# A new beginning for a hybrid decoder layer: early x and weights, unread products, a pinned first norm, and the keys' products on VectorE

## The chip, the cores and the metric

One core of a Trainium2 chip runs the whole kernel. The metric is the device time of one execution in microseconds (us). Engines: TensorE (PE, matmuls), VectorE (DVE), ScalarE (ACT), GpSimd (POOL) and SyncE (SP, which only issues DMAs here). Each engine takes its instructions in its own order and waits for the others through semaphores.

## The reference

One step of one decoder layer on 256 prompt positions and 8 samples of 4 tokens: N = 288 columns in all. D = 2048, all in float32.

```python
h = _rmsnorm(x, norm_pre_mix)
z = h @ w_in                              # shift | pool | gate a | gate b columns
zs_mix = zs + (prev - zs) * mu_shift      # token shift
ya, new_wkv = _rwkv7_branch(zs_mix, ...)  # matrix state per head, 16 heads of 64
yb, new_pool = _pool_branch(zp, ...)      # means over windows of 2, 4, 8, 16, then pool_w
m = sigmoid(zga) * (ya @ w_branch_a) + sigmoid(zgb) * (yb @ w_branch_b)
x = x + _rmsnorm(m @ w_out, norm_post_mix)
f, new_conv = _conv_ffn(_rmsnorm(x, norm_pre_ffn), ...)   # gate and up of 5632, conv of 3, gelu
x = x + _rmsnorm(f, norm_post_ffn)
```

The outputs are x for prompt and samples, and the new shift, matrix, pooling and conv states of both.

## The kernel before

**Dense products.** Activations lie transposed: 16 tiles of 128 channels by 288 columns. Each dense product takes 128 x 128 weight tiles and is made as three matmuls of rounded halves (`three`): high weight by high x (L263), high weight by low x (L264), low weight by high x (L265). The halves are exact splits: the high one is a rounded copy, the low one the rest. Weights come in *units* of four tiles, 256 KB: `load_to` issues their DMA on SP's queue into `raw` (seven buffers); `split_to` makes `whi` on ACT (L202) and `wlo` on DVE (L203), four buffers each. `take` keeps the splits three units ahead of the products and the loads six more. A unit is 12 matmuls.

**The start.** The first norm's factor per column (rstd) is applied after the products, so products can begin before it is known. `first_parts(k)` makes the halves of x part k, `xh` (ACT, with the norm's weight g1 from the table `vec`) and `xl` (DVE). `first_squares(k)` squares part k on ACT and adds it to `acc` on POOL; `rstd_of` turns `acc` into rstd by a product with ones and a RECIPROCAL on DVE. Meanwhile `dense_together(seq_lo, ...)` runs five products side by side: units 0 to 4 use x parts 0 to 3, units 5 to 9 parts 4 to 7, and so on, 20 units in all, 240 matmuls. `x_load(q)` loads x parts 4q to 4q+3. `vec` (165.5 KB) and the constants `con` (557.5 KB: identity, ones, masks, eps) come on ACT's queue.

**Side work.** Everything that isn't a dense product is written as generators in three lanes; `advance` takes one step of every lane after each unit, and a half step of lane 2 within a unit. `startup` is the first of lane 1. Then for four groups g of four heads `front(g)` makes the RWKV operands (`cum`, the decay's cumulative sums; `AR`; `KB`, products of keys `kq` and of `tha`, the second operand, with the inverse decay `eN`, at L621; `rr`), and `late(g)` with `inverse` does the chunked recurrence: `Gm` by TensorE and DVE, `Gm*wr` on POOL, written to DRAM as `dA` by POOL's queue, read back as `Ab` by SP's queue, then a triangular inverse on DVE into `wt`, whose product `W` goes through DRAM again (`dW`) and is transposed on DVE (`tq`), for the products `ps_q`, `ps_x` (S), `ps_s` (UV) and `ps_u` (X). Lane 3 makes the pooling branch, `zb`, window sums `win` on POOL, `d` on DVE, its halves `dh` and `dl`, and the branch's `ybh`, `ybl`.

**The second norm.** `rstd_spread` turns sums of squares into a factor spread over 128 partitions: `ps_sum` on TensorE, a square root on ACT, `rq` and the diagonal `dg` on DVE, `ps_spread` on TensorE. It is called for `rst2` between the output product and the feed-forward.

**Order.** A scheduler that simulates the program sets each engine's order by its own estimate, except for instructions wrapped in `pin`, which keep the order in which they are written on their engine. So an edit in one place can move rows elsewhere.

Of the kernel before, what the change touches and what calls it, by code (L numbers as in the profile page):

```python
# [10 lines left out]
F32 = mybir.dt.float32  # L11
# [7 lines left out]
P = 128  # L19
D = 2048  # L20
KD = D // P
# [18 lines left out]
UK = 4  # L40
AHEAD = 3
FA = 2
TOG = 3
BT = 5
IWAIT = 3
# [62 lines left out]
def hybrid_step(ctx: ExitStack, tc: tile.TileContext, t):  # L108
# [69 lines left out]
    def load_to(u):  # L178
        while cursor["load"] <= min(u, len(units) - 1):
            i = cursor["load"]  # L180
            if i in (4, 4 + 5, 4 + 10):
                x_load((i - 4) // 5 + 1)
            ap, nk = units[i]
            m = ap.shape[2]
            w = wp.tile([P, UK, P], F32, tag="raw", name="raw", bufs=7)
            if i:
                nc.sync.dma_start(out=w[:, :nk, :m], in_=ap)
            raw[i] = w
            cursor["load"] += 1
# [127 lines left out]
    con = cst.tile([P, NCON], F32, name="con")  # L317
    xe = ExitStack()
    xr_p = xe.enter_context(tc.tile_pool(name="xr", bufs=1, side="right"))
    nc.scalar.dma_start(out=vec, in_=t["vec"])  # L320
    first = cst.tile([P, 1], F32, name="first")
    dve.memset(first, 0.0)
    act.activation(out=first, in_=first, func=AF.Square)
    nc.scalar.dma_start(out=con, in_=t["con"])
    xr = []

    def x_load(q):
        xq = xr_p.tile([P, 4, N], F32, name=f"xr{q}")
        xr.extend(xq[:, i] for i in range(4))
        if q == 0:  # L330
            load_to(0)
            nc.sync.dma_start(out=xq[:, 0:2], in_=t["xT"][:, 0:2, :])
            nc.sync.dma_start(out=raw[0][:, 0:4], in_=units[0][0][:, 0:4])
            nc.sync.dma_start(out=xq[:, 2:4], in_=t["xT"][:, 2:4, :])
            load_to(1)
        else:
            for h in range(0, 4, 2):
                nc.sync.dma_start(out=xq[:, h:h + 2], in_=t["xT"][:, 4 * q + h:4 * q + h + 2, :])
# [7 lines left out]
    def c_(name):  # L346
        o, w = CON[name]
        return con[:, o:o + w]
# [19 lines left out]
    def rstd_of(sums, name, where):  # L368
        ps = psb.tile([P, 512], F32, tag="s", name="ps_rstd")
        for i, a in enumerate(sums):  # L370
            pe.matmul(ps[:, :N], ones, a, start=i == 0, stop=i == len(sums) - 1)
        r = where.tile([P, N], F32, tag=f"rstd_{name}", name=f"rstd_{name}")
        act.activation(out=r, in_=ps[:, :N], func=AF.Sqrt, scale=1.0 / D, bias=c_("eps"))
        dve.reciprocal(r, r)
        return r

    TC = N // 3

    def rstd_spread(sums, where, between=()):

        ps = psb.tile([P, 3, 2], F32, tag="s", name="ps_sum")
        for i, a in enumerate(sums):
            for c in range(3):
                pin(pe.matmul(ps[0:TC, c], a[:, c * TC:(c + 1) * TC], ones[:, 0:2],
                              start=i == 0 and c == 0, stop=i == len(sums) - 1 and c == 2))
            if i < len(between):
                between[i]()
        q = where.tile([TC, 3, 1], F32, tag="rq", name="rq")
        pin(act.activation(out=q, in_=ps[0:TC, :, 0:1], func=AF.Sqrt, scale=1.0 / D, bias=c_("eps")[0:TC]))
        pin(dve.reciprocal(q, q))  # L390
        dg = where.tile([TC, 3, TC], F32, tag="dg", name="dg")
        pin(dve.tensor_tensor(
            dg, ident[0:TC, 0:TC].unsqueeze(1).to_broadcast([TC, 3, TC]), q.to_broadcast([TC, 3, TC]), op=ALU.mult
        ))
        pr = psb.tile([P, 512], F32, tag="s", name="ps_spread")
        pin(pe.matmul(pr[:, :N], ones[0:TC], dg.rearrange("p c t -> p (c t)"), start=True, stop=True))
        return pr[:, :N]


# [4 lines left out]
    def first_parts(k):  # L404
        xh[k], xl[k] = scaled_parts(k, xr[k], v_("g1", k))

    def first_squares(k):
        if k == 0:
            act.activation(out=acc, in_=xr[0], func=AF.Square)
            return  # L410
        sq = xr_p.tile([P, N], F32, tag="sq", name="sq", bufs=3)
        act.activation(out=sq, in_=xr[k], func=AF.Square)
        pool.tensor_tensor(acc, acc, sq, op=ALU.add)

    def startup():
        for k in range(4, KD, 2):
            first_parts(k)
            first_parts(k + 1)
            yield
        for k in range(KD):  # L420
            first_squares(k)
            if k % 2:
                yield
        norms["mix"] = rstd_of([acc], "mix", cst)

    first_parts(0)
    split_to(0)
# [104 lines left out]
    def front(g, rr, kx, vv, lora):  # L532
# [82 lines left out]
        KBs = kp.tile([P, G, 2, 32], F32, tag="KBs", name="KBs")  # L615
        rh = kp.tile(W2, F32R, tag="t0", name="rh")
        rl = kp.tile(W2, F32R, tag="t3", name="rl")
        for par in range(2):
            for eng, src, flip in ((dve, kq, 0), (pool, bb, 1)):
                h, slot = HALF[par], par ^ flip  # L620
                ins = eng.tensor_tensor(  # L621
                    KB[h, :, :, slot, :].rearrange("p c g t -> p g c t"),
                    src[h, :, :TP].rearrange("p g (c t) -> p g c t", c=NCH),
                    eN[h, :, :TP].rearrange("p g (c t) -> p g c t", c=NCH),
                    op=ALU.mult,
                )
                if eng is dve:
                    pin(ins)
            if not par:
                yield  # L630
        for slot, src in enumerate((kq, bb)):
            pool.tensor_tensor(KBs[:, :, slot, :], src[:, :, TP:], eN[:, :, TP:], op=ALU.mult)
        ready[g] = (vv, AR, KB, KBs, wr, dch, dsm)
# [21 lines left out]
    def late(g):  # L655
# [65 lines left out]
        S0 = kp.tile([P, G, NB, C], F32, tag="S0", name="S0")  # L721
        nc.sync.dma_start(out=S0, in_=t["st_wkv"][:, p0:p0 + G])
        def inverse():
            yield 2 * IWAIT
            pin(dve.memset(Ab.rearrange("p a b -> p (a b)")[:, 0:1024:33], 1.0))
            wt = kp.tile([P, 2, 8, 32], F32, tag="inv", name="wt")
            Wb, tmp = wt[:, 0], wt[:, 1]
            dve.tensor_copy(Wb, c_("inv0").rearrange("p (a b) -> p a b", a=8))
            work = 0
            for tt in range(1, 32):  # L730
                n = tt + 1
                dve.tensor_tensor(  # L732
                    tmp[:, :, :n], Wb[:, :, :n], Ab[:, :n, tt].unsqueeze(1).to_broadcast([P, 8, n]), op=ALU.mult
                )
                dve.tensor_reduce(out=Wb[:, :, tt], in_=tmp[:, :, :n], op=ALU.add, axis=AX.X)
                work += 120 + 16 * n
                if work >= IWORK:
                    yield work // IWORK
                    work %= IWORK
            WQ.dma_start(  # L740
                out=dW.rearrange("q (r i) t -> (q r) (i t)", r=4), in_=Wb.rearrange("p i t -> p (i t)")
            )
# [249 lines left out]
        lane3.todo.append(finish())  # L992

    bones_r = zp_.tile([P, P], F32R, name="bones_r")
    act.copy(out=bones_r, in_=c_("bones"))
    mB = [dmb.tile([P, N], F32, tag=f"mB{j}", name=f"mB{j}") for j in range(16)]
    tga = [dmb.tile([P, N], F32, tag=f"tga{j}", name=f"tga{j}") for j in range(16)]

# [218 lines left out]
        act.activation(out=o, in_=ps[:, :N], func=AF.Copy, scale=v_("g2", j))  # L1217
        og.append(o)
    me.close()
    rst2 = rstd_spread([acc2, sq], ep)  # L1220
    acc3 = ep.tile([P, N], F32, tag="accn3", name="acc3")
    xh, xl = [None] * KD, [None] * KD

# [258 lines left out]
```

## Time and profile before

| What | Value |
|---|---|
| Time, median of 3 runs | 1649.15 us (1648.79 to 1650.57) |
| The profiled execution | 1651.69 us, span 1649.6 us |
| Mean granted clock of TensorE | 0.992 |
| Busy: PE, DVE, ACT, POOL | 1611.8 (98%), 1103.4 (67%), 816.8 (50%), 369.7 (22%) us |
| DMA | 278.96 MB, mean 169 GB/s |
| Chain that ended last | PE 86%, DVE 4%, DMA 2% |

The profile is of one execution; 2.1 us of its time lie outside the span. A row of instructions names line, engine, operation, output and inputs; "[2.22 <-DMA raw<-in_w_in]" says that the engine stood idle for 2.22 us before it, until that event. The granted clock is 1.00 at full speed. Busy time of TensorE includes matmuls that run slowly.

### The profile page before, as it was taken

The page shows a single profiled execution, that of the slowest core. Times are in us where ns is not written, and L with a number is a line of the kernel's source. Part 1 is how long each engine was busy: PE and PEld are TensorE (multiplying, and loading weights), DVE is VectorE, ACT ScalarE, POOL GpSimd, SP SyncE. Part 2 cuts the span into 40 slices and gives each one's busy share as a digit, 9 for nine tenths or more (in the row PEclk, how much of TensorE's full clock was granted, in tenths as well). Part 3 has the DMA queues.
Part 4 walks back from the last instruction along what each step waited for, and adds up shares of the span by engine and source line. Part 5 has one row for each costly group of instructions (what it writes and reads, how often), then busy time and mean ns, then how long its engine had stood idle before and what let it go on. Part 6 is the DMA issues. An engine that isn't in the chain of part 4 may idle for free.

```text
span 1649.6 us, 35997 instructions
## 1 busy us (share of the span) xinstructions
PE 1611.8 (98%) x13540; PEld 1577.3 (96%) x13540; DVE 1103.4 (67%) x2217; ACT 816.8 (50%) x1521; POOL 369.7 (22%) x612
## 2 busy tenths in 40 slices
PE   6989999999999999999999999999999999999998
PEld 6989989989989999999899999999999999999998
DVE  6788887888878766645876664446666555666654
ACT  5544445445435445545655554445555433455554
POOL 4574352343332112300211110001111000111111
PEclk9999999999999999999999999999999999999999
DMA  7535546546545648755355555555555555555553
GB/s 241 161 120 165 170 142 200 161 122 190 157 155 181 187 155 288 229 166 190 108 163 167 167 165 167 166 167 165 168 167 166 166 166 167 166 167 167 176 167 108
DMA packets 157230, 278.96 MB, mean 169 GB/s; under 512 B 25584, under 2 KB 32240, under 8 KB 157056
## 3 DMA queue, kind: packets, MB, share of 16 engines
q1 hardware_dynamic: 151104, 259.16, 50.8%
q0 software_dynamic: 5664, 16.77, 2.9%
q8 instruction: 106, 1.74, 0.4%
q10 hardware_dynamic: 288, 0.74, 0.1%
q14 instruction: 68, 0.56, 0.1%
HBM read 262.67 MB, written 13.93 MB: 168 GB/s over the span
## 4 chain that ended last, share of the span: by engine, by line
PE 86%; DVE 4%; DMA 2%; issue 1%; POOL 0%; ACT 0%; SPq 0%; DVEq 0%; POOLq 0%; ACTq 0%
PE acc L265 27%; PE acc L263 27%; PE acc L264 27%; DVE wlo L203 1%; DMA dW<-wt 1%; PE ps_g L671 0%; DVE xl L357 0%; DVE og L1229 0%; PE ps_s L909 0%; DMA W<-dW 0%; PE ps_u L899 0%; PE ps_x L888 0%; PE ps_y L1353 0%; DVE cum L577 0%; DMA raw<-in_w_in 0%
## 5 line engine op out<-in xcount | busy, mean ns | idle before, releaser
L203 DVE TENSOR_TENSOR wlo<-raw,whi 128x512 fp32r<-128x512 f32 x928 | 661.1, 715 | 415.2 <-ACT whi L202 406.7
L202 ACT CAST whi<-raw 128x512 fp32r<-128x512 f32 x928 | 572.0, 620 | 680.6 <-PE acc L264 629.7
L263 PE MATMUL acc<-xh,whi 128*128 128x288 f32 x2736 | 814.3, 298 | 14.5 <-ACT whi L202 8.8
L265 PE MATMUL acc<-xh,wlo 128*128 128x288 f32 x2736 | 811.4, 297 | 7.0 <-DVE wlo L203 7.0
L264 PE MATMUL acc<-xl,whi 128*128 128x288 f32 x2736 | 812.7, 297 | 0.0
L263 PEld LDWEIGHTS acc<-xh,whi 128*128 128x128 f32 x2736 | 517.4, 189 | 17.9 <-ACT whi L202 9.2
L265 PEld LDWEIGHTS acc<-xh,wlo 128*128 128x128 f32 x2736 | 520.2, 190 | 12.0 <-DVE wlo L203 8.9
L264 PEld LDWEIGHTS acc<-xl,whi 128*128 128x128 f32 x2736 | 520.6, 190 | 2.0 <-issue 0.9
L265 PE MATMUL acc<-ah,wlo 128*128 128x288 f32 x704 | 208.7, 296 | 0.0
L263 PE MATMUL acc<-ah,whi 128*128 128x288 f32 x704 | 208.0, 296 | 0.0
L264 PE MATMUL acc<-al,whi 128*128 128x288 f32 x704 | 205.2, 292 | 0.0
L1266 POOL COPY cout<-gt 128x2 f32<-128x2 f32 x44 | 31.1, 706 | 597.2 <-DVE gt L1262 575.9
L264 PEld LDWEIGHTS acc<-al,whi 128*128 128x128 f32 x704 | 134.2, 191 | 0.0
L263 PEld LDWEIGHTS acc<-ah,whi 128*128 128x128 f32 x704 | 132.2, 188 | 0.0
L265 PEld LDWEIGHTS acc<-ah,wlo 128*128 128x128 f32 x704 | 131.9, 187 | 0.0
L1274 POOL TENSOR_TENSOR cv<-cv,rstd_ffn 128x288 f32<-128x288 f32 x44 | 36.2, 823 | 74.5 <-ACT cv L1273 73.6
L732 DVE TENSOR_TENSOR wt<-wt,Ab 128x16 f32<-128x16 f32 (+30 forms) x124 | 51.4, 414 | 1.8
L462 POOL TENSOR_TENSOR df<-zt 128x256 f32<-128x256 f32 (+1 forms) x27 | 22.7, 840 | 91.6 <-DVE zt L460 85.6
L1270 DVE SCALAR_TENSOR_TENSOR cv<-gt,vec,cv 128x255 f32<-128x255 f32 x88 | 43.0, 489 | 0.0
L263 PE MATMUL acc<-ybh,whi 128*128 128x288 f32 x128 | 38.6, 301 | 0.0
L265 PE MATMUL acc<-ybh,wlo 128*128 128x288 f32 x128 | 38.4, 300 | 0.0
L264 PE MATMUL acc<-ybl,whi 128*128 128x288 f32 x128 | 38.1, 298 | 0.0
(308 smaller groups left out, 1539.8 us busy)
## 6 DMA issues: line engine op xcount, KB each, us to landing
raw<-in_w_ffn_in SPq DMA_DIRECT2D x352, 256.0 KB, 3.0
raw<-in_w_in SPq DMA_DIRECT2D x264, 256.0 KB, 3.5
raw<-in_w_ffn_out SPq DMA_DIRECT2D x176, 256.0 KB, 2.7
raw<-in_w_out SPq DMA_DIRECT2D x64, 256.0 KB, 3.0
raw<-in_w_branch_b SPq DMA_DIRECT2D x32, 256.0 KB, 3.2
raw<-in_w_branch_a SPq DMA_DIRECT2D x32, 256.0 KB, 3.9
xr<-in_xT SPq DMA_DIRECT2D x8, 288.0 KB, 5.6
tga<-th POOLq DMA_DIRECT2D x16, 144.0 KB, 3.7
```

The source lines that it names most:

```text
L202: act.copy(out=hi[:, a:b, :m], in_=w[:, a:b, :m])
L203: dve.tensor_tensor(lo[:, a:b, :m], w[:, a:b, :m], hi[:, a:b, :m].bitcast(F32), op=ALU.subtract)
L263: pe.matmul(ps, hi, xh, start=start, stop=False)
L264: pe.matmul(ps, hi, xl, start=False, stop=False)
L265: pe.matmul(ps, lo, xh, start=False, stop=stop)
L462: pool.tensor_tensor(df[:m, :TP], zt[:m, 0:TP], zt[:m, 1:ZB], op=ALU.subtract)
L732: dve.tensor_tensor(tmp[:, :, :n], Wb[:, :, :n], Ab[:, :n, tt].unsqueeze(1).to_broadcast([P, 8, n]), op=ALU.mult)
L1266: pool.tensor_copy(cout[:, f, 0:2], gt[:, TP - 2:TP])
L1270: dve.scalar_tensor_tensor(cv[:, s:TP], gt[:, 0:TP - s], w, cv[:, s:TP], op0=ALU.mult, op1=ALU.add)
L1274: pool.tensor_tensor(cv, cv, rst3, op=ALU.mult)
```

## The change

- **Unread products.** POOL clears a 128 x 128 tile; TensorE's queue begins with eleven float32 products of it (`WARM`), whose output nothing reads. `keep_busy(n)` puts n such products (ones by identity) into `rstd_spread`, 5 ahead of the spread and 8 behind it, for `rst2`.
- **The first loads.** Of `vec` only the 16 columns of g1 come on ACT's queue; the other 315 columns and `con` move to SP's queue, behind the weights of unit 6. On SP's queue x part 0 comes alone, then the weights of unit 0, then x part 1, then 2 and 3.
- **The first norm.** `startup` makes one x part and one square per step, pinned, in 16 steps; before, it made two parts a step for six steps and then two squares a step, unpinned.
- **KB.** All four products of a group are on DVE, pinned, with a step of the lane between them; before, the two of `tha` were on POOL.
- **Two small ones.** For group 0 `inverse` begins two half steps later; the rounded copy of a constant, `bones_r`, is pinned.

```diff
+WARM = 11
@@ load_to
+            if i == 7:
+                nc.sync.dma_start(out=vec[:, KD:], in_=t["vec"][:, KD:])
+                nc.sync.dma_start(out=con, in_=t["con"])
@@
-    nc.scalar.dma_start(out=vec, in_=t["vec"])
+    nc.scalar.dma_start(out=vec[:, 0:KD], in_=t["vec"][:, 0:KD])
...
-    nc.scalar.dma_start(out=con, in_=t["con"])
@@ x_load
-            nc.sync.dma_start(out=xq[:, 0:2], in_=t["xT"][:, 0:2, :])
+            nc.sync.dma_start(out=xq[:, 0:1], in_=t["xT"][:, 0:1, :])
             nc.sync.dma_start(out=raw[0][:, 0:4], in_=units[0][0][:, 0:4])
+            nc.sync.dma_start(out=xq[:, 1:2], in_=t["xT"][:, 1:2, :])
             nc.sync.dma_start(out=xq[:, 2:4], in_=t["xT"][:, 2:4, :])
@@
+    def keep_busy(n):
+
+        ps = psb.tile([P, 512], F32, tag="s", name="ps_busy")
+        for _ in range(n):
+            pin(pe.matmul(ps[:, 0:P], ones, ident, start=True, stop=True))
+
-    def rstd_spread(sums, where, between=()):
+    def rstd_spread(sums, where, between=(), busy=()):
...
+        if busy:
+            keep_busy(busy[0])
         q = where.tile([TC, 3, 1], F32, tag="rq", name="rq")
...
         pin(pe.matmul(pr[:, :N], ones[0:TC], dg.rearrange("p c t -> p (c t)"), start=True, stop=True))
+        if busy:
+            keep_busy(busy[1])
@@ first_squares
-            act.activation(out=acc, in_=xr[0], func=AF.Square)
+            pin(act.activation(out=acc, in_=xr[0], func=AF.Square))
...
-        act.activation(out=sq, in_=xr[k], func=AF.Square)
+        pin(act.activation(out=sq, in_=xr[k], func=AF.Square))
@@ startup
-        for k in range(4, KD, 2):
-            first_parts(k)
-            first_parts(k + 1)
+        for k in range(KD):
+            if k < KD - 4:
+                first_parts(k + 4)
+                pin(last_hi[0])
+                pin(last[0])
+            first_squares(k)
             yield
-        for k in range(KD):
-            first_squares(k)
-            if k % 2:
-                yield
         norms["mix"] = rstd_of([acc], "mix", cst)
+
+    zero = xr_p.tile([P, P], F32, name="zero")
+    pool.memset(zero, 0.0)
+    warm0 = psb.tile([P, 512], F32, tag="s", name="ps_warm")
+    for _ in range(WARM):
+        pin(pe.matmul(warm0[:, :P], zero, zero, start=True, stop=True))
@@ front
-        for par in range(2):
-            for eng, src, flip in ((dve, kq, 0), (pool, bb, 1)):
+        for src, flip in ((kq, 0), (bb, 1)):
+            for par in range(2):
                 h, slot = HALF[par], par ^ flip
-                ins = eng.tensor_tensor(
+                pin(dve.tensor_tensor(
                     KB[h, :, :, slot, :].rearrange("p c g t -> p g c t"),
...
-                if eng is dve:
-                    pin(ins)
-            if not par:
-                yield
+                if (flip, par) != (1, 1):
+                    yield
@@ inverse
-            yield 2 * IWAIT
+            yield 2 * IWAIT + (0 if g else 2)
@@
-    act.copy(out=bones_r, in_=c_("bones"))
+    pin(act.copy(out=bones_r, in_=c_("bones")))
@@
-    rst2 = rstd_spread([acc2, sq], ep)
+    rst2 = rstd_spread([acc2, sq], ep, busy=(5, 8))
```

The order on VectorE in the first norm, before: low halves of x (xl) and of weights (wlo).

```order
L203 TENSOR_TENSOR wlo<-raw,whi 128x512 x3
L203 TENSOR_TENSOR wlo<-raw,whi 128x4x96
L357 SCALAR_TENSOR_TENSOR xl_233<-xr_111,vec,xh_232 128x288
L357 SCALAR_TENSOR_TENSOR xl_237<-xr_111,vec,xh_236 128x288
L357 SCALAR_TENSOR_TENSOR xl_257<-xr_111,vec,xh_256 128x288
L357 SCALAR_TENSOR_TENSOR xl_261<-xr_111,vec,xh_260 128x288
L357 SCALAR_TENSOR_TENSOR xl_281<-xr_124,vec,xh_280 128x288
L357 SCALAR_TENSOR_TENSOR xl_285<-xr_124,vec,xh_284 128x288
L357 SCALAR_TENSOR_TENSOR xl_305<-xr_124,vec,xh_304 128x288
L357 SCALAR_TENSOR_TENSOR xl_309<-xr_124,vec,xh_308 128x288
L203 TENSOR_TENSOR wlo<-raw,whi 128x512 x4
```

The same engine now, from x part 4 on, with the `der` steps (small ones on `vec`) between.

```order
L361 SCALAR_TENSOR_TENSOR xl_201<-xr_98,vec,xh_200 128x288
L207 TENSOR_TENSOR wlo<-raw,whi 128x512
L361 SCALAR_TENSOR_TENSOR xl_222<-xr_98,vec,xh_221 128x288
L467 TENSOR_SCALAR der<-vec 128x8
L207 TENSOR_TENSOR wlo<-raw,whi 128x512
L468 TENSOR_SCALAR der<-vec 128x8
L469 TENSOR_SCALAR der<-vec 128x8
L470 TENSOR_SCALAR der<-vec 128x8
L361 SCALAR_TENSOR_TENSOR xl_245<-xr_98,vec,xh_244 128x288
L207 TENSOR_TENSOR wlo<-raw,whi 128x512
L361 SCALAR_TENSOR_TENSOR xl_268<-xr_98,vec,xh_267 128x288
L207 TENSOR_TENSOR wlo<-raw,whi 128x4x96
```

The runs of four and eight x halves are split up: one x half and one weight half now take turns until the last x part, with the `der` steps behind the eleventh of the halves.

VectorE at the keys' products of group 0, before.

```order
L586 TENSOR_TENSOR thw<-cum,thw 128x576
L610 TENSOR_TENSOR AR<-rr,eP 128x576
L203 TENSOR_TENSOR wlo<-raw,whi 128x512
L608 SCALAR_TENSOR_TENSOR AR<-kkr,thw 128x576
L203 TENSOR_TENSOR wlo<-raw,whi 128x512 x2
L621 TENSOR_TENSOR KB<-kq,eN 64x2x4x64
L1026 TENSOR_TENSOR zb<-acc,rstd_mix 128x256
L1027 TENSOR_TENSOR zb<-acc,rstd_mix 128x32
L203 TENSOR_TENSOR wlo<-raw,whi 128x512 x2
```

VectorE at the same place now.

```order
L207 TENSOR_TENSOR wlo<-raw,whi 128x512 x2
L641 TENSOR_TENSOR KB<-kq,eN 64x2x4x64
L1044 TENSOR_TENSOR zb<-acc,rstd_mix 128x256
L1045 TENSOR_TENSOR zb<-acc,rstd_mix 128x32
L207 TENSOR_TENSOR wlo<-raw,whi 128x512
L1061 SCALAR_TENSOR_TENSOR d<-win_1388,zb 128x256
L1064 SCALAR_TENSOR_TENSOR d<-win_1388,zb 128x32
L1068 TENSOR_TENSOR d<-win_1388,con 128x15
L1069 TENSOR_TENSOR d<-d,zb 128x15
L370 TENSOR_TENSOR dl<-d,dh 128x288
L641 TENSOR_TENSOR KB<-kq,eN 64x2x4x64
L207 TENSOR_TENSOR wlo<-raw,whi 128x512
```

The two products of `tha` follow right behind these rows, one per weight half, and are gone from POOL's queue. The steps of the pooling branch (zb, d, dl) stand earlier among the products: one zb pair is now behind a single KB, as before, but the other stands ahead of `AR`.

VectorE at the transposes of group 2, before.

```order
L203 TENSOR_TENSOR wlo<-raw,whi 128x512
L852 STREAM_TRANSPOSE tq<-W 32x256
L569 TENSOR_SCALAR wr<-ps_ns 32x1 x2
L565 TENSOR_SCALAR wr<-ps_n 128x8
L569 TENSOR_SCALAR wr<-ps_n 32x1 x2
L577 SCALAR_TENSOR_TENSOR cum<-con,thw 128x256 x2
L579 COPY cum<-thw 128x2x8
L566 RECIPROCAL wr<-wr 128x8
L852 STREAM_TRANSPOSE tq<-W 32x256
```

VectorE at the transposes of group 2 now.

```order
L589 TENSOR_SCALAR wr<-ps_ns 32x1 x2
L585 TENSOR_SCALAR wr<-ps_n 128x8
L589 TENSOR_SCALAR wr<-ps_n 32x1 x2
L597 SCALAR_TENSOR_TENSOR cum<-con,thw 128x256
L586 RECIPROCAL wr<-wr 128x8
L590 RECIPROCAL wr<-wr 32x2 x2
L597 SCALAR_TENSOR_TENSOR cum<-con,thw 128x256
L599 COPY cum<-thw 128x2x8
L1114 TENSOR_TENSOR th<-acc,rstd_mix 128x288
L870 STREAM_TRANSPOSE tq<-W 32x256
```

The first transpose stood ahead of the cumulative sums; it now stands behind them and behind a step of the gates (th).

More of the change, by code (lines that the diff above doesn't have):

```diff
@@ L625, in front @@
                     op=ALU.mult,
-                )
-                if eng is dve:
-                    pin(ins)
-            if not par:
-                yield
+                ))
+                if (flip, par) != (1, 1):
+                    yield
         for slot, src in enumerate((kq, bb)):
```

## The prediction

> **What bounds the kernel now.** I read the engine totals first, then what TensorE waited for, then short windows around each wait, for the granted clock. The first fence has the page's span and totals (share of the span, instructions), the second TensorE's waits (line, releaser: us in all, times, longest).
>
> ```profile
> span 1649.6 us, 35997 instructions
> ...
> PE 1611.8 (98%) x13540; PEld 1577.3 (96%) x13540; DVE 1103.4 (67%) x2217; ACT 816.8 (50%) x1521; POOL 369.7 (22%) x612
> ```
> ```profile
> PE acc L263 <- ACT whi L202: 8.8, 1, 8.8
> PE acc L265 <- DVE wlo L203: 7.6, 6, 3.3
> PE acc L263 <- DVE zb L1027: 4.1, 1, 4.1
> PE ps_u L899 <- ACT X L894: 2.8, 1, 2.8
> PE ps_q L858 <- DVE tq L852: 2.8, 4, 0.8
> PE acc L263 <- ACT xh L356: 1.6, 1, 1.6
> PE acc L263 <- ACT dh L363: 1.4, 1, 1.4
> PE ps_x L888 <- DVE S L915: 1.3, 1, 1.3
> PE ps_s L909 <- DVE UV L902: 1.2, 1, 1.2
> ```
>
> TensorE is busy for 1611.8 of 1649.6 us, so only 37.8 us are idle, and the nine waits above make 31.6 of them. Nothing in the change takes a product away from the reference's work. It can gain only from these waits and from matmuls that run slowly behind them. The next rows (stretch, its length, TensorE's busy time and matmuls, granted clock, DMA share, GB/s) show the first 33 us and then the later places (18.90 to 25.84, busy throughout, is left out).
>
> ```profile
> 0.00:8.83 8.83, 0.00 (x0) 1.00 0.75 235
> 8.83:12.27 3.44, 3.44 (x13) 1.00 1.08 383
> 12.27:17.51 5.24, 5.24 (x39) 1.00 1.07 383
> 17.51:18.90 1.39, 0.00 (x1) 1.00 1.05 387
> ...
> 25.84:29.14 3.30, 0.00 (x1) 1.00 0.00 1
> 29.14:32.76 3.62, 3.62 (x16) 0.53 0.56 170
> ```
> ```profile
> 101.68:105.76 4.08, 0.00 (x1) 0.84 0.56 180
> 105.76:111.00 5.24, 5.24 (x22) 0.50 0.21 72
> 145.34:148.60 3.26, 3.26 (x15) 0.51 0.73 206
> 457.40:462.20 4.80, 4.80 (x22) 0.50 0.58 183
> 789.60:791.96 2.36, 0.75 (x2) 0.69 0.24 86
> 791.96:796.45 4.49, 4.49 (x19) 0.50 0.00 0
> ```
>
> A matmul at full speed takes 5.24/39 = 0.134 us; behind the long waits it takes 0.24 (5.24/22, 4.80/22, 4.49/19). At 8.83 a like 0.26 (3.44/13) stands beside a printed clock of 1.00, so I take the matmuls' pace as the evidence there. The excess over 0.134 a matmul is 1.7 us at 8.83, 1.5 at 29.14, 2.3 at 105.76, 1.2 at 145.34, 1.9 at 457.40 and 1.9 at 791.96: 10.5 us in all, that the idle figure doesn't contain.
>
> **The start.** These rows are of the timeline (start, length, engine, line), then the DMA rate in 40 slices of the first 20 us, and groups by line (minimum, median and maximum ns, first and last start).
>
> ```profile
> 8.16 0.62 ACT L202 CAST whi<-raw 128x512 fp32r<-128x512 f32 x1 [2.22 <-DMA raw<-in_w_in]
> 21.68 6.80 DVE L357 SCALAR_TENSOR_TENSOR xl<-xr,vec,xh 128x288 fp32r<-128x288 f32 x8
> 28.40 2.48 DVE L203 TENSOR_TENSOR wlo<-raw,whi 128x512 fp32r<-128x512 f32 x4
> ```
> ```profile
> GB/s 0 0 0 55 96 267 339 300 231 220 213 285 371 399 424 372 363 343 362 385 382 406 386 386 394 389 352 355 384 376 388 415 378 384 400 383 390 369 164 107
> ```
> ```profile
> L356 ACT ACTIVATE xh<-xr,vec x16: 518/522/535, 5.0 to 22.1; 128x288 fp32r<-128x288 f32 x16
> L357 DVE SCALAR_TENSOR_TENSOR xl<-xr,vec,xh x16: 504/1049/1067, 5.5 to 28.0; 128x288 fp32r<-128x288 f32 x16
> L413 POOL TENSOR_TENSOR acc<-acc,sq x15: 790/905/1215, 5.2 to 26.4; 128x288 f32<-128x288 f32 x15
> L203 DVE TENSOR_TENSOR wlo<-raw,whi x12: 677/680/1299, 8.8 to 30.2; 128x512 fp32r<-128x512 f32 x10, 128x384 fp32r<-128x384 f32 x2
> ```
>
> The first weights land at 8.16 because vec and con (723 KB on ACT's queue) and both early x parts share the rate with them. Summed over its half microseconds, the rate has moved 0.53 MB by 4 us and 1.0 MB by 6. With 16 columns of vec, 144 KB of x and then 256 KB of weights ahead, I put the landing at 4.1 to 4.7 and the first product at 5.2, 3.6 earlier. The third and fourth x parts end 0.83 MB of SP's queue and, with POOL's 0.23 MB beside it, come near 6.2, and VectorE makes their low halves by 7.7. So unit 0 (12 products, 1.6 us) is stretched to about 8.0: 1.2 us of new waiting.
>
> From then on the old order puts eight low halves in one piece (6.80 us from 21.68) ahead of four weight halves; TensorE runs dry behind it for 3.30. In the new order they alternate. A pair costs VectorE 6.80/8 + 2.48/4 = 1.47 us, up to 1.05 + 0.68 = 1.73, against 12 x 0.134 = 1.61 of TensorE for a unit: balanced, so the 1.39 and 3.30 go, and I allow 0.5 for single late halves. ACT's three steps a unit (weight half 0.62, x half 0.52, and a square of the same size as the x half) are 1.66 at most, near TensorE's 1.61; I count no wait for them. The eleven zero products are queued ahead; each is narrower than a 288-column f32 product of two instructions, 0.75 us in the spread's row below, so 128 columns make 0.33, and eleven 3.7, from about 1.2: 4.9, before the weights. (That row's clock was 0.69; at 0.50 they are 0.46 each and end at 6.3, 1.1 late: the bound.) The clock is then up at the first product: 1.7 saved; and with 3.30 gone, its 1.5.
>
> Lost before: 8.83 + 1.7 + 1.39 + 3.30 + 1.5 = 16.7. Lost after: 5.2 + 1.2 + 0.5 = 6.9. The norm's rstd comes three units later in the order, and its consumers with it; I charge 0.5. The start gives **-9.3**. Moving vec's rest and con behind raw6 on SP's queue puts 720 KB, 1.9 us at 0.38 MB/us, ahead of raw7; that unit isn't wanted before 5.2 + 1.2 + 7 x 1.6 = 17.6, and by the rate the 3.8 MB up to it are in at 13.5. VectorE's der steps wait for vec's rest and hold the halves behind them; they stand behind 11 halves, and I expect both near 12 to 13. The squares, pinned one a step, add nothing on ACT's path.
>
> By the Trainium skill (TensorE: Matmul & The Clock Gate, Part 1: The HAM clock gate), the array runs at half clock until it has been busy for a free-running window of about 3.4 us, and cools after an idle one of that length. The trace agrees with the length (slow stretches of 3.26 to 5.24) but not with the threshold: 1.61 us of waiting at 791.96 is followed by 0.50, 1.39 at 17.51 is not. By the rule alone a gap as short as the second norm's would not cool the array, the last term below would be nothing, and the sum 1632.
>
> **Keys' products on VectorE.** The two POOL products per group become VectorE's; the rest moves with the order.
>
> ```profile
> L621 POOL TENSOR_TENSOR KB<-tha,eN x8: 1269/1616/1802, 102.8 to 452.8; 64x512 f32<-64x512 f32 x8
> L621 DVE TENSOR_TENSOR KB<-kq,eN x8: 676/928/1953, 103.4 to 457.3; 64x512 f32<-64x512 f32 x8
> 129.25 2.36 POOL L688 DMA_DIRECT2D dA<-Gm  x4
> 140.67 0.09 DVE L725 MEMSET Ab<- 128x32 f32 x1 [3.22 <-DMA Ab<-dA]
> 443.38 0.44 DVE L852 STREAM_TRANSPOSE tq<-W 32x256 f32<-32x256 f32 x1 [3.71 <-DMA W<-dW]
> ```
>
> Eight more on VectorE at 0.68 to 0.93 are 5.4 to 7.4 us, on an engine that is 67% busy: hidden, where its look-ahead is whole. POOL, 22% busy, loses 8 x 1.6. In group 0, TensorE waits 4.08 for zb, which stands behind two wlo and a KB, then loses 2.3 to the clock; of the 2.9 that are left of its waits for wlo beside 1.39 and 3.30, I put 1.2 here: 7.6. In the new order one zb stands a unit earlier and the KBs are spread; most of it goes. But Ab's memset blocks VectorE until Ab has landed (3.22), and the chain Gm, dA, Ab comes forward less than TensorE does, so dh's wait (1.4, and 1.2 of slow clock) grows by about 3; new waits near d and ybl take about 1. Net **-3.5**, between 0 and -6.5.
>
> For groups 1 to 3 the waits for tq, X, S and UV are 8.1, with 1.9 of slow clock: 10.0. In the new order the transposes around 443 stand behind the decay's cumulative sums, so the 3.71 of VectorE's blocking is used, and the 2.8 and 1.9 at 457 should go. The others are reshuffled rather than removed. Net **-4**, from -9 to +3.
>
> **Second norm.** Five and eight unread products fill TensorE's waits of 1.04 and 1.61 at
>
> ```profile
> 789.60 0.75 PE L396 MATMUL ps_spread<-dg,con 96*128 96x288 f32 x2 [1.04 <-DVE dg L392]
> ```
>
> At 0.33 they take 1.7 and 2.7, up to 0.6 and 1.0 longer than the waits; at a full clock I take 0.25, so 1.25 and 2.0, 0.6 over. The 1.9 of slow clock go; unless VectorE, busy with og, x and xl, is then the limit. Net **-1.5**, from 0 to -1.9.
>
> Sum: -9.3 - 3.5 - 4 - 1.5 = -18.3. The profiled execution took 1651.69, with 2.1 outside its span, and gives 1633.4; on the median of 1649.15 it is 1630.9, and I forecast 1631.
>
> **The rivals.** *The first norm is paced by VectorE and POOL.* If each pinned pair meets a POOL addition and costs the two maxima, 1.07 + 1.30 = 2.37, twelve pairs are 9.1 us over TensorE's 1.61, nearly the whole gain of the start: 1640. For it: the medians of xl (1.05 against 0.50 at best) while POOL adds. Against: the wlo's median is its minimum. By the Trainium skill (SBUF — State Buffer, SBUF: two separate sides), a VectorE step with two SBUF inputs and a GpSimd step that reads there shut each other out for the whole instruction. By that rule a pair is 0.50 + 0.68 + 0.905 = 2.09, twelve are 5.8 us over, and the sum gives 1637; the xl row agrees, the wlo row doesn't. Chance 0.12.
>
> *Given back later.* The reshuffled queues make as many new waits in the four groups as they remove, so that only the start and the second norm count: 1649.15 - 10.8 = 1638. The group chains hang on DMA round trips (dA issued at 129.25, Ab in by 140.67), that a faster TensorE doesn't shorten. Chance 0.18.
>
> *The unread products don't hold the clock,* because zeros or the short fillings count for nothing. Then 1.7 and 1.5 come back: 1634. For it: the printed 1.00 beside slow matmuls at 8.83, so what governs the pace there isn't seen. Chance 0.06.
>
> *Slower.* KB's last two on VectorE push Gm, dA and Ab back in every group, VectorE blocks at each memset as at 140.67, and TensorE drains: a 4.08 wait and 2.3 of slow clock as at 101.68, in each group. That is 6.4 a group beyond what the groups lose now. Against the 10.8 of start and second norm it decides from 2.7 a group (3.5 to be measurable); at 6.4 in all four it gives 1649.15 - 10.8 + 25.6 = 1664. Against it: VectorE idle for a third of the span. Chance 0.04.
>
> **How the numbers follow.** The forecast has 0.60, its own range 1625 to 1636. The 0.2% that a measurement here can tell from no change are 3.3 us. 1634, 1638 and 1640 are all faster by more than that, 0.96 with the forecast; 0.03 of it I give to sums that nearly cancel, where "given back" is larger than I put it. Faster 0.93, same 0.03, slower 0.04. For the low end the groups reach their -9 (5 more), group 0 half of its further 3 and the start loses 1.7 less to new waits: 1623. The high end takes in both middle rivals, with 1 us over 1640.
>
> **What would show it.** First product near 5.2 us, at 0.13 from its start; no wait over 1 us between 9 and 35; the first norm's RECIPROCAL some 9 us earlier. TensorE's wait for zb gone and that for dh at about 4; the X wait near 450 gone; no 0.50 stretch behind the second norm. The forecast is wrong if der or con holds a queue at the start, if wlo's pairs run at 2 us or more, or if a group shows a new wait above 4 us.

## The result, and the profile after

The changed kernel takes 1634.85 us in the median (1632.01 to 1637.87, four runs), the kernel before beside it 1649.86 (1648.79 to 1651.35). The ratio is 0.9909, with a 95% interval of 0.9889 to 0.9929: faster by 15.0 us. The profiled execution took 1634.87, its span is 1633.1, 16.5 under the span before. First the page's rows and TensorE's waits in the changed kernel (line, releaser: us in all, times, longest). Lines have moved: L267 to L269 are the three matmuls, L206 and L207 the weight splits.

```profile
span 1633.1 us, 36103 instructions
...
PE 1612.4 (99%) x13588; PEld 1577.6 (97%) x13588; DVE 1101.9 (67%) x2225; ACT 816.8 (50%) x1521; POOL 355.7 (22%) x605
```
```profile
PE acc L267 <- DVE zb L1045: 3.3, 1, 3.3
PE ps_q L876 <- DVE tq L870: 2.4, 4, 1.3
PE acc L269 <- DVE wlo L207: 2.0, 3, 1.5
PE acc L267 <- DVE gt L1280: 2.0, 1, 2.0
PE ps_warm L444 <- POOL zero L441: 1.0, 1, 1.0
PE ps_w L267 <- ACT zwa_h L367: 0.9, 1, 0.9
PE acc L268 <- DVE dl L370: 0.9, 2, 0.6
PE acc L267 <- ACT whi L206: 0.8, 1, 0.8
PE ps_w L268 <- DVE zwa_l L370: 0.8, 1, 0.8
```

The waits for X (2.8), for dh (1.4) and for xh in the second norm (1.6) are gone or under 0.3; that for zb is nearly as long as before (3.3 against 4.1); those for gt, zwa_h and zwa_l are new. Four stretches of TensorE follow (length, busy time and matmuls, granted clock, DMA share, GB/s).

```profile
0.00:6.06 6.06, 4.21 (x22) 1.00 0.63 154
6.06:8.90 2.84, 2.33 (x9) 1.00 1.07 368
8.90:46.30 37.40, 35.59 (x262) 1.00 0.75 255
46.30:55.40 9.10, 7.37 (x41) 0.81 0.44 131
```

The first product starts at 6.06 instead of 8.83, behind 4.21 us of zero products and a last wait. From 8.90 to 46.30 only 1.8 us are idle, where the kernel before lost 3.30 in one piece, and 1.5 of them are one wait that ends at 46.30. There a new bad stretch begins: 9.10 us with 1.7 idle, and a granted clock of 0.81.

To see where the time lies, I summed TensorE's lost time from the two traces, row by row: idle time, and for the weight products the excess of a start-to-start distance between 0.17 and 0.30 us over 0.1325. A stage is bounded by the weight unit whose high half ACT then makes, so that the same work is compared. "Net" counts the time of the unread products with what is lost after (4.2 us at the start; 2.7 in the second norm, the waits of 1.04 and 1.61 that they fill).

| Units | What runs there | Lost before | Lost after | Net | Forecast |
|---|---|---|---|---|---|
| 0 to 31 | first norm and what follows | 16.5 | 8.3 | -4.0 | -9.3 |
| 32 to 79 | group 0 | 12.5 | 8.5 | -4.0 | -3.5 |
| 80 to 394 | groups 1 to 3 and the branches | 24.8 | 17.9 | -6.9 | -4 |
| 395 to 449 | second norm | 6.3 | 2.8 | -0.8 | -1.5 |
| 450 on | feed-forward | 0.5 | 0.5 | 0 | 0 |

The lost time falls from 60.5 to 37.9; less 6.9 of unread products that is 15.7 of the 16.5 between the spans.

### The profile page after: what moved, and what is told of

Its sections match the earlier page's. It is cut to its first block, busy times and chain, and to the rows that moved or that the text cites. A ratio compares the mean times of both kernels' runs of the same rounds, so it can differ in the third digit from the quotient of the medians.

```text
span 1633.1 us, 36103 instructions
## 1 busy us (share of the span) xinstructions
PE 1612.4 (99%) x13588; PEld 1577.6 (97%) x13588; DVE 1101.9 (67%) x2225; ACT 816.8 (50%) x1521; POOL 355.7 (22%) x605
## 4 chain that ended last, share of the span: by engine, by line
PE 90%; DVE 4%; DMA 2%; issue 2%; ACT 1%; POOL 0%; SPq 0%; DVEq 0%; ACTq 0%; POOLq 0%
PE acc L269 28%; PE acc L267 28%; PE acc L268 28%; DVE wlo L207 1%; DMA W<-dW 1%; DMA dW<-wt 1%; PE ps_g L689 1%; DVE wt L750 0%; PE ps_s L927 0%; DVE cum L597 0%; DMA lora<-in_lora 0%; DMA xr<-in_xT 0%; PE ps_u L917 0%; PE ps_x L906 0%; PE ps_y L1371 0%
## 5 line engine op out<-in xcount | busy, mean ns | idle before, releaser
L207 DVE TENSOR_TENSOR wlo<-raw,whi 128x512 fp32r<-128x512 f32 x928 | 656.9, 711 | 401.8 <-ACT whi L206 394.9
L206 ACT CAST whi<-raw 128x512 fp32r<-128x512 f32 x928 | 572.6, 619 | 661.8 <-PE acc L268 617.1
L267 PE MATMUL acc<-xh,whi 128*128 128x288 f32 x2736 | 811.1, 297 | 6.1 <-DVE zb L1045 3.3
L269 PE MATMUL acc<-xh,wlo 128*128 128x288 f32 x2736 | 809.5, 296 | 2.0 <-DVE wlo L207 2.0
L269 PEld LDWEIGHTS acc<-xh,wlo 128*128 128x128 f32 x2736 | 517.7, 189 | 5.8 <-DVE wlo L207 2.9
L267 PEld LDWEIGHTS acc<-xh,whi 128*128 128x128 f32 x2736 | 514.4, 188 | 8.9 <-issue 6.5
L269 PE MATMUL acc<-ah,wlo 128*128 128x288 f32 x704 | 208.7, 296 | 0.0
L267 PE MATMUL acc<-ah,whi 128*128 128x288 f32 x704 | 208.1, 296 | 0.0
L267 PEld LDWEIGHTS acc<-ah,whi 128*128 128x128 f32 x704 | 132.2, 188 | 0.0
L269 PEld LDWEIGHTS acc<-ah,wlo 128*128 128x128 f32 x704 | 131.9, 187 | 0.0
L1288 DVE SCALAR_TENSOR_TENSOR cv<-gt,vec,cv 128x255 f32<-128x255 f32 (+1 forms) x88 | 43.4, 494 | 0.3 <-ACT cv L1281 0.3
L267 PE MATMUL acc<-ybh,whi 128*128 128x288 f32 x128 | 38.7, 303 | 0.0
L269 PE MATMUL acc<-ybh,wlo 128*128 128x288 f32 x128 | 38.1, 298 | 0.0
```

The source lines that it names most:

```text
L206: act.copy(out=hi[:, a:b, :m], in_=w[:, a:b, :m])
L207: dve.tensor_tensor(lo[:, a:b, :m], w[:, a:b, :m], hi[:, a:b, :m].bitcast(F32), op=ALU.subtract)
L267: pe.matmul(ps, hi, xh, start=start, stop=False)
L269: pe.matmul(ps, lo, xh, start=False, stop=stop)
L1288: dve.scalar_tensor_tensor(cv[:, s:TP], gt[:, 0:TP - s], w, cv[:, s:TP], op0=ALU.mult, op1=ALU.add)
```

## Experiments

Each ratio is against the kernel before on the same chip. "Over" or "under the changed kernel" is the difference of two medians that were not taken side by side: the kernel before took 1649.86 beside the changed kernel and 1650.32 to 1650.74 beside the runs below, so up to 0.9 us of it need not be the edit's. "Stage" means the same sums as in the table.

### The first norm's old steps

```diff
-        for k in range(KD):
-            if k < KD - 4:
-                first_parts(k + 4)
-                pin(last_hi[0])
-                pin(last[0])
-            first_squares(k)
+        for k in range(4, KD, 2):
+            first_parts(k)
+            first_parts(k + 1)
             yield
+        for k in range(KD):
+            first_squares(k)
+            if k % 2:
+                yield
```

The squares lose their `pin` too.

> The changed kernel with the old steps of the first norm: two x parts a step for six steps, then two squares a step, nothing pinned. My theory: the pinned alternation is what takes the waits of 1.39 and 3.30 us and the slow stretch behind them out, but it also delays the last square, the release of the x tiles' memory, lora's load that waits for it, and with lora ScalarE and rstd. So without it TensorE is about 5 us later at unit 18 and gets 4 to 6 of them back by 62 us: 1634 to 1637 (the changed kernel has 1634.85), with ScalarE's wait of 4.1 us for lora gone. Rival, the alternation is the larger part of the start's gain and lora's wait has another cause: 1640, with that wait still there.

Measured: 1639.45, ratio 0.9934 (0.9919 to 0.9950), 4.6 over the changed kernel. ACT's wait for lora is gone, as the theory has it. These rows are of the timeline (start, length, engine, line): the changed kernel's, then the kernel before's, then this one's.

```profile
35.55 1.28 SPq L1021 DMA_DIRECT2D lora<-in_lora  x1
37.62 0.65 PE L375 MATMUL ps_rstd<-acc,con 128*128 128x288 f32 x2
40.97 0.41 ACT L367 CAST lo_h<-lora 128x256 fp32r<-128x256 f32 x1 [4.12 <-DMA lora<-in_lora]
43.74 1.95 DVE L378 RECIPROCAL rstd_mix<-rstd_mix 128x288 f32<-128x288 f32 x1 [1.12 <-ACT rstd_mix L377]
```
```profile
31.29 0.42 SPq L1003 DMA_DIRECT2D lora<-in_lora  x1
41.41 0.65 PE L371 MATMUL ps_rstd<-acc,con 128*128 128x288 f32 x2
43.93 1.95 DVE L374 RECIPROCAL rstd_mix<-rstd_mix 128x288 f32<-128x288 f32 x1 [1.12 <-ACT rstd_mix L373]
```
```profile
30.32 0.38 SPq L1022 DMA_DIRECT2D lora<-in_lora  x1
32.50 0.65 PE L375 MATMUL ps_rstd<-acc,con 128*128 128x288 f32 x2
34.77 1.95 DVE L378 RECIPROCAL rstd_mix<-rstd_mix 128x288 f32<-128x288 f32 x1 [1.12 <-ACT rstd_mix L377]
```

In the changed kernel TensorE hands over the sum of squares at 38.3, but ACT stands at the copy of lora until 40.97, ahead of a weight half, a table load and the square root; RECIPROCAL starts at 43.74, where it did before. With the old steps it starts at 34.77. Two things go against each other here. At unit 18 the old steps are 3.8 late (ACT makes its high half at 35.98 instead of 32.21), near the theory's 5, though the wait of 3.30 isn't back: the longest for wlo is 1.0. But by the end of the first stage they have lost 2.9 less. The time is still longer: zb's one wait grows from 3.3 to 5.4, those for tq from 2.4 to 5.4 in all.

```profile
PE acc L267 <- DVE zb L1046: 5.4, 1, 5.4
PE ps_q L877 <- DVE tq L871: 5.4, 5, 2.2
```

So the new steps gain in the first norm and lose more than that to the late rstd; that the whole time is better with them comes from the groups. Why the groups lose more behind an earlier rstd these rows don't say.

### The old loads

The first `dma_start` lines are those of before: vec and con on ACT's queue, x parts 0 and 1 in one piece.

> The changed kernel with the old first loads: vec and con whole on ScalarE's queue at the start, x parts 0 and 1 in one piece ahead of the first weights. My theory: the first product starts near 8.8 instead of 6.06, 2.8 us later, but rstd is paced by lora's landing, so that no more than 1 to 2 us of it are left in the time: 1636 to 1637. Rival, everything behind starts that much later: 1637.7 or more. Rival, con's early arrival helps, nothing is lost: 1634.

Measured: 1637.83, ratio 0.9919 (0.9902 to 0.9935), 3.0 over the changed kernel, with overlapping intervals; its span is 3.8 over. Its first product:

```profile
8.45 0.61 PE L264 MATMUL acc<-xh,whi 128*128 128x288 f32 x1 [3.20 <-ACT whi L203]
```

It starts 2.39 later, and the first stage loses 2.1 more. By the median the rival with the full loss is the nearer one. The profiled execution can't settle it: about 1.4 of its 3.8 lie in the second norm, which the edit doesn't touch (the last section has the reason). The row shows one thing more: the zero products ended 3.20 us before, and the weight products behind that wait run slowly until 14.55, with 2.1 us of excess.

### No unread products at the start

```diff
-    for _ in range(WARM):
-        pin(pe.matmul(warm0[:, :P], zero, zero, start=True, stop=True))
```

> The changed kernel without the eleven unread products at the beginning of TensorE's queue. My theory: the first 12 to 16 matmuls run at 0.24 us instead of 0.13 for some 3.4 us, up to 1.7 us lost at unit 0, of which part is hidden by its waits for the low halves of x, and later by rstd: 1635 to 1636. Rival, the clock costs the full 1.7 and it stays: 1636.5. Rival, the products' pace has nothing to do with them: 1634.8 and the first matmuls as in the changed kernel.

Measured: 1633.75, ratio 0.9904 (0.9884 to 0.9923); 1.1 under the changed kernel, within the intervals.

```profile
6.11 0.61 PE L267 MATMUL acc<-xh,whi 128*128 128x288 f32 x1 [6.11 <-ACT whi L206]
6.51 0.44 PE L268 MATMUL acc<-xl,whi 128*128 128x288 f32 x1
```

Without them the first products run at 0.24 to 0.44 apart until 10.0 us, but they wait for the x halves one by one anyway. With them, products run 0.13 apart from 8.80 on, so the third guess, that the pace has nothing to do with them, is not borne out. In the time the eleven products bring nothing that can be measured.

### No unread products in the second norm

The call is `rstd_spread([acc2, sq], ep)` again.

> The changed kernel without the 5 and 8 unread products around the second norm's spread. My theory: the stretch at half clock behind the norm (1.9 to 2.2 us) comes back, but the new wait of 2.00 us for gt on VectorE some 45 us later goes, since VectorE paces that phase: 1635 to 1636, 0.5 to 1 over the changed kernel. Rival, the two have nothing to do with each other: 1637, with the half-clock stretch and the wait for gt both there.

Measured: 1636.40, ratio 0.9911 (0.9892 to 0.9929), 1.5 over the changed kernel, again with overlapping intervals. The slow stretch without them, and the same place with them (the second fence, with the products in its first row):

```profile
779.00:785.00 6.00, 6.00 (x26) 0.52 0.00 0
```
```profile
772.90:776.60 3.70, 3.70 (x32) 1.00 0.30 105
776.60:781.50 4.90, 4.88 (x36) 1.00 0.02 3
```

They keep the clock at 1.00: 26 matmuls in 6.00 us without, 36 in 4.90 with. They delay nothing: from the last sums of squares to the first product behind the norm it is 4.08 us in both profiles. The wait for gt of 2.0 is gone in this run, as the theory has it. With the products 2.4 us of slow clock go, and that wait takes most of them back; by the sums 0.8 remain. In the medians the gain isn't resolved.

### Keys' products back on POOL

`front` is that of before, with two of the four products on POOL.

> The changed kernel with the keys' products as before: two of each group on VectorE, two on POOL. My theory: KB's move to VectorE and the order that comes with it are what takes the waits for dh (1.4 and 1.2 of slow clock) in group 0 and for X (2.8 and 1.9) in group 3 out; without it 4 to 7 us come back: 1639 to 1642. Rival, those waits went because rstd and the lanes stand at other units now, whatever makes KB: 1634 to 1636. Rival, VectorE loses by the products it took over: 1632.

Measured: 1645.92, ratio 0.9971 (0.9961 to 0.9981), 11.1 over the changed kernel: more than any guess. TensorE's waits in this run:

```profile
PE ps_q L878 <- DVE tq L872: 5.1, 4, 2.2
PE acc L267 <- ACT dh L367: 3.8, 3, 1.9
```

Group 0 loses 11.8 instead of 8.5, and units 80 to 209 lose 13.9 instead of 8.6: the waits for dh and tq are back. The wait for X, which the theory had coming back too, is 0.6 us here against 2.8 in the kernel before, so it does not hang on the keys' products alone. About 1.5 us more are lost in the second norm, where the edit does nothing (see the last section).

### Keys' products alone

The kernel before with `front` of the changed one, and nothing else.

> The kernel before with one part of the change: all four of a group's keys' products on VectorE, pinned, a step of the lane between them. My theory after putting them back on POOL cost 11 us: this part alone is the larger half of the gain, since POOL is free for the steps that the chain to Ab waits for and VectorE's own steps no longer run beside POOL's; 1638 to 1641 (before 1649.9), with the start as before. Rival, KB's move pays only together with the early rstd and the inverse's later step: 1645 to 1648.

Measured: 1641.57, ratio 0.9951 (0.9932 to 0.9970): 8.7 under the kernel before. This one part makes the larger half of the gain. By the sums above, 3.0 come from group 0, 2.0 from units 80 to 209, and 2.9 from units 210 to 239, where the transposes stand at another place. The profiled spans differ by 10.1, of which two parts lie where the edit does nothing: the first product at 7.86 instead of 8.83, and 1.3 in the second norm. What the move costs VectorE shows in the products themselves (count, busy time, mean ns; the kernel before, then the changed one):

```profile
L621 POOL TENSOR_TENSOR KB<-tha,eN 64x512 f32<-64x512 f32 x8 | 12.6, 1569 | 0.3
L621 DVE TENSOR_TENSOR KB<-kq,eN 64x512 f32<-64x512 f32 x8 | 8.7, 1090 | 0.1
```
```profile
L641 DVE TENSOR_TENSOR KB<-kq,eN 64x512 f32<-64x512 f32 x8 | 7.3, 908 | 0.1
L641 DVE TENSOR_TENSOR KB<-tha,eN 64x512 f32<-64x512 f32 x8 | 5.7, 707 | 0.1
```

VectorE makes eight products more in 4.3 us more. Yet its busy time falls in both pairs of kernels that differ by this edit alone, from 1103.4 (the kernel before) to 1102.2 (this run), and from 1103.7 (keys' products back on POOL) to 1101.9 (the changed kernel). Two of the four are shown above; these are this run's and that with the products back on POOL.

```profile
PE 1612.1 (98%) x13540; PEld 1577.6 (96%) x13540; DVE 1102.2 (67%) x2225; ACT 817.0 (50%) x1521; POOL 354.8 (22%) x604
PE 1619.1 (99%) x13588; PEld 1583.7 (96%) x13588; DVE 1103.7 (67%) x2217; ACT 816.3 (50%) x1521; POOL 370.5 (23%) x613
```

So its other steps win back more than that, while 12.6 us of POOL's work no longer run beside them. By the Trainium skill (SBUF — State Buffer, Who interferes with whom), a VectorE step with two inputs in SBUF and a GpSimd step that reads there contend. These rows agree: the products of `kq` took 1090 ns in the mean with POOL's beside them, 908 without.

That is why the move is cheap; it isn't shown to be where 8.7 us come from. The edit does three things: it moves two products of each group to VectorE, it pins them, and it puts two more steps of the lane into each group. Two such steps in group 0 alone change the time by 11.5 us below (Keys later in group 0). No run moves the products without the steps, so the shares of the engine and of the order stay open. That POOL is free earlier for the chain to Ab isn't seen in group 0: POOL issues dA at 129.25 before and at 128.6 here, with the first product 0.97 earlier.

### lora's copy held back

The last argument pins ACT's copy for group 0, which puts it at 71.4 us instead of 40.97.

```diff
-        exact_parts(lo_h, lo_l, lora)
+        exact_parts(lo_h, lo_l, lora, g == 0)
```

> The changed kernel with ScalarE's copy of lora for group 0 held behind the group's first products with the keys (about ten units later), so that it no longer stands ahead of rstd's square root. My theory: ScalarE's wait of 4.1 us for lora goes, RECIPROCAL starts near 40 instead of 43.7, and the waits of 1.51, 0.94 and 0.79 and the slow stretch of 1.2 behind them go: 1630 to 1632. Rival, lora isn't the cause (rstd is paced by the squares and the table load): 1635, with RECIPROCAL near 43. Rival, it is the cause, but the gain is given back in the groups' chains: 1633 to 1635 with an early RECIPROCAL.

Measured: 1632.33, ratio 0.9886 (0.9870 to 0.9903), the lowest of all, 2.5 under the changed kernel with intervals that overlap. Its span is 0.6 lower. RECIPROCAL, and the two waits that grew:

```profile
40.06 1.96 DVE L378 RECIPROCAL rstd_mix<-rstd_mix 128x288 f32<-128x288 f32 x1 [1.12 <-ACT rstd_mix L377]
```
```profile
PE ps_q L876 <- DVE tq L870: 4.3, 5, 1.8
PE acc L267 <- DVE zb L1045: 4.2, 1, 4.2
```

lora's copy is what held rstd: without it RECIPROCAL starts 3.7 earlier, and the first stage loses 3.8 less. In the profiled execution units 32 to 394 lose 4.2 more, 0.9 of it at zb and 1.9 at tq. That is the third guess; the median lies between the first and the third.

### Squares two a step

From the fifth step on, `startup` makes two squares a step; x parts as changed.

> The changed kernel with the squares two a step from the fifth step on, so that POOL's last addition and with it the release for lora's load come some 6 us earlier; x parts as changed. My theory: lora lands before ScalarE wants it, RECIPROCAL starts near 38, and 3 to 5 us are gained by 62 us, less up to 1.5 that VectorE loses beside a busier POOL: 1631 to 1633. Rival, the denser additions slow each pair on VectorE to 2 us, and the waits for wlo return near 20: 1636 or more.

Measured: 1640.31, ratio 0.9942 (0.9928 to 0.9957), 5.5 over. My account of lora's delay was wrong: POOL's last addition ended 2.9 earlier (31.65 against 34.56), and lora was still late.

```profile
34.76 0.38 SPq L1027 DMA_DIRECT2D lora<-in_lora  x1
39.82 0.41 ACT L367 CAST lo_h<-lora 128x256 fp32r<-128x256 f32 x1 [3.87 <-DMA lora<-in_lora]
```

In SP's order lora stands behind 26 weight loads in the changed kernel, behind 25 here, 20 with the old steps and 19 before. Here it is issued right behind six weight loads that end at 34.66, three us after POOL is done. So the release of its memory isn't the bound; its place in the queue is. The old loads, without vec and con on this queue, leave it behind 26; the old steps of the first norm put it back to 20. It is the new steps, then, that moved lora, and not the longer queue. The rest of this run's loss lies in the groups: zb's wait is 5.4 us, where the changed kernel has 3.3. About 1.5 are the second norm's, which the edit doesn't touch.

### The old first wait of the inverse

`yield 2 * IWAIT` for group 0 too.

> The changed kernel with the old first wait of the inverse in group 0 (six half steps instead of eight). My theory: VectorE's memset of Ab stands a unit earlier and blocks 1.6 to 2 us longer for Ab's landing, and a wait of TensorE for dh or d near 140 comes back: 1636 to 1638. Rival, VectorE has the slack there: 1635.

Measured: 1637.03, ratio 0.9918 (0.9897 to 0.9940), 2.2 over with overlapping intervals; the span is 1.7 over. VectorE's block at the memset of Ab in group 0 is shorter than the changed kernel's 1.99, not longer:

```profile
137.07 0.09 DVE L743 MEMSET Ab<- 128x32 f32 x1 [1.18 <-DMA Ab<-dA]
```

So my mechanism isn't there. Part of the profile's difference lies ahead of the edit: lora landed at 42.41 instead of 40.89, and RECIPROCAL started 1.5 later. Whether the step matters stays open.

### Keys later in group 0

```diff
+        if g == 0:
+            yield 2
         for src, flip in ((kq, 0), (bb, 1)):
```

> The changed kernel with the second of these edits alone: in group 0 the keys' products two steps later, zb ahead of them. My theory: the wait for zb (3.25 us and 2.36 of slow clock behind it) shrinks by 1 to 3 us, since two wlo stand ahead of zb still, and group 0's later keys cost under 1: 1632 to 1634. Rival, the later keys put Gm, dA and Ab back, and VectorE blocks at Ab's memset: 1637.

Measured: 1646.36, ratio 0.9981 (0.9967 to 0.9995), 11.5 over the changed kernel. Its ten executions spread widely, from 1642.90 to 1652.84; the profiled one took 1649.75, so the sizes below are of a longer one than the median.

```profile
PE acc L269 <- DVE wlo L207: 4.3, 8, 1.5
PE ps_q L878 <- DVE tq L872: 4.0, 3, 2.6
PE acc L267 <- DVE tga L1187: 3.6, 2, 1.8
PE acc L267 <- DVE zb L1047: 2.1, 1, 2.1
```

The wait for zb shrinks by 1.2, as the theory has it. But two steps of the lane in group 0 move the groups behind it: group 3's `ps_u` starts at unit 294 instead of 281, and its end now meets the branch products (tga, new; 7.6 us lost in units 300 to 394, where the changed kernel loses 0.1). The rival had the sign; Ab's memset isn't its way, since it blocks only 2.2 us in all four groups.

### Both edits, with and without the first unread products

The copy of lora held back and the later keys together, and the same without the eleven products.

> The changed kernel with two edits: ScalarE's copy of lora for group 0 pinned behind the keys, and in group 0 two steps of the lane more before the keys' products, which in VectorE's order puts zb ahead of the first of them. My theory: the wait for zb (4.17 us and 1.3 of slow clock with the first edit alone) shrinks to under 1, and half of it stays in the time, since the groups' round trips through DRAM don't move with TensorE: 1628 to 1631. Rival, all of it is given back in the groups: 1632 as with the first edit alone.

> The changed kernel with both of these edits and without the eleven unread products at the start. My theory: they save 0.4 to 0.9 us of slow matmuls in unit 0, which waits for the low halves of x anyway, so the time is that of the kernel with both edits, within 1 us. Rival, with rstd no longer late the slow matmuls at the start count: 1 to 2 us more.

Measured: 1641.06, ratio 0.9948 (0.9929 to 0.9968), and 1643.03, ratio 0.9952 (0.9938 to 0.9966). The later keys cost 8.7 beside the early rstd too, with the same waits for tga (3.9), and the wait for zb is 3.4 in the first profile instead of the expected 1. The two differ by 2.0, within their intervals, so the unread products stay unresolved here.

## Why the prediction was right, and where not

The forecast was 1631 and a gain of 18; measured are 1634.85 and a gain of 15.0. The sign and the bound are as argued: TensorE's work is the same, and the gain is lost time that goes. That the time lies in the range is in part luck: the start gained 5.3 less than its term, the groups 3.4 more than theirs, and the two errors offset each other. Of the signs that I had named, the X wait, the half clock behind the second norm and the quiet stretch from 9 to 35 came as said. The first product's time and pace, RECIPROCAL, zb and dh did not.

- **First product at 5.2, measured 6.06.** The zero products were done at 5.21, 0.3 behind the sum's 4.9 and well ahead of the bound of 6.3; the weights were the later, by 0.85. The pace of 0.13 came only at 8.80: until then the products waited for the halves one by one.
- **The alternation on VectorE.** The 3.30 and the 1.39 went, and no wait above 0.3 us stands between 9 and 35. VectorE and POOL didn't pace the norm: that rival is out. With the old steps the 3.30 is gone too, so it was not the alternation alone that took it; the alternation is worth 3.8 us at unit 18.
- **"rstd comes three units later, I charge 0.5".** This step failed. The first 32 units gained 4.0 instead of 9.3, though unit 16 was reached 9.5 us earlier (ACT makes its high half at 28.7 instead of 38.3). rstd came only 0.2 earlier: the new steps had moved lora's load seven weight loads down SP's queue, and ACT stood 4.12 us at its copy. Behind that TensorE lost 1.51, 0.94 and 0.79 and 1.2 of slow clock, 4.4 of the 5.3 that the start fell short; 0.9 are the later first product. I followed vec and con along that queue, and not the small load. The sign "RECIPROCAL some 9 us earlier" did not even fit my own three units, which are 4.8 us: with lora held back it came 3.9 earlier, and 9.2 only with the old steps.
- **Keys on VectorE.** The sum of the two terms was -7.5, measured -10.9, and the keys alone make 8.7 of gain in their own run. I priced the added products on VectorE (5.4 to 7.4; those of `tha` take 5.7) and gave nothing for what its other steps gain when POOL is silent, nor for the two more steps of the lane. How the 8.7 divide among these isn't shown. Inside group 0 I was wrong twice with opposite signs: the wait for zb stayed (3.25 and 2.4 of slow clock), and dh's, which I had growing by 3, went to 0.2.
- **Transposes behind the cumulative sums.** The waits near 457 for X went as read from the order.
- **Second norm -1.5, measured -0.8 by the stages (the run without it: 1.5 in the medians, not resolved).** The products fitted the waits and the clock stayed up, but 2.0 came back as a wait for gt: VectorE is the limit 45 us on, as the step allowed and its size did not.
- **Unread products.** The rival that they don't hold the clock is out: 1.00 with them and 0.52 without in the second norm, 0.13 and 0.24 apart from 8.8 to 10.0 at the start. What the clock was worth in the time is resolved in neither place.
- **"Given back later".** As a rival it was too strong: the groups gained. But what the runs gained at the start, by the old steps or by lora's copy, was lost again there.

## What to carry to other kernels

When an order is made by a planner, look up the new place of every DMA on a queue, the small ones above all, also where the edit only changes the steps of an engine. Here a load that moved back by seven weight loads stopped ScalarE, which takes its steps in order, and its next steps made the factor that everything waits for. Moving elementwise work off GpSimd can cost VectorE less than the work's own time, as here: compare VectorE's busy time in two kernels that differ by that alone. Judge a gain at the start by the end: in two runs here the groups lost it again.

## What was not expected of the hardware

The same wait is followed by half clock in one run and by full clock in another. Behind the wait of 2.0 us for gt, the changed kernel (first row) and the one with the keys on POOL (second) show:

```profile
817.76:822.00 4.24, 4.24 (x32) 1.00 0.41 145
```
```profile
826.92:831.00 4.08, 4.08 (x19) 0.58 0.46 158
```

32 matmuls against 19 in the same time, a loss of 1.6 us. Of the eleven profiled kernels that have this wait of 2.0 us, five show the slow stretch behind it and six don't, and none of their edits is in this place. By the Trainium skill (TensorE: Matmul & The Clock Gate, Part 1: The HAM clock gate), the activity window runs free of the kernel, and the clock falls after an idle time of about 3.4 us. The two rows agree with the first; not with the second, since 2.0 us were enough in the second row. A single profile's difference of 1.5 us can be this alone.
